# A two-layer RWKV-7 and S5 trunk on one core: the learning rate and the gated unit keep the tanh of their sigmoids, and the half and the offset go into constants and weights

## The chip, the core and the metric

The kernel runs on one core of a Trainium2 chip. A core has a matrix engine (TensorE; PE in the profile, its weight loads PEld), a vector engine (VectorE, DVE), an activation engine (ScalarE, ACT), a general engine (GpSimd, POOL) and a queue that here issues nearly all of the DMAs (SyncE, SP). Each engine runs its own instructions in order and waits on semaphores for the others. The metric is the device time of one execution in microseconds (us), less being better.

## The reference

The input is one sequence of 1024 frames with 1024 features, in float32. Layer 0 mixes over time with RWKV-7, layer 1 with a diagonal complex state-space model and a gated linear unit; each mixer is followed by a squared-ReLU MLP of width 4096, and each of the four sub-layers by a layer norm of sqrt(2)·x + f(x). Cut to what the change touches:

```python
# layer 0, the time mixer
a = jax.nn.sigmoid(a0 + (xa @ a1) @ a2)          # the learning rate
kk = heads(k * k_k)
kk = kk / jnp.maximum(jnp.sqrt(jnp.sum(kk * kk, axis=-1, keepdims=True)), 1e-12)
k = k * (1.0 + (a - 1.0) * k_a)
seq_in = (rh, wh, kh, vh, -kk, kk * ah)
# state = state * w + (state @ a_t) b_t + v k, with a_t = -kk and b_t = kk * a
...
# layer 1, the gated unit
z = y @ w_glu
return z[..., :d] * jax.nn.sigmoid(z[..., d:])
```

## The kernel before

Features lie on the 128 partitions (8 tiles of 128, `KT`), frames on the free axis, in two halves of 512 (`HT`; H is the half). Every large product is made of three float32r products: an operand is split into a high part, a float32r copy that ScalarE makes (`split`, L153), and a low part, the difference, made by VectorE (L154). `mm3` (L201) issues high·high, high·low and low·high. The weights pass through `wload` (L167): a DMA into `wraw`, of which there are two buffers, then the split into `whi` and `wlo`, of which there are three each. The products collect in three PSUM banks (`psd`).

The kernel makes its sigmoids from tanh, as sigmoid(z) = 0.5·tanh(z/2) + 0.5. ScalarE computes the tanh with a scale of 0.5, and a second pass makes the half and the offset.

The time mixer has these steps.

- `rwkv_proj(H)` makes the projections of a half. In it `rates(n)` (L393) makes feature tile n of the decay `sg` and of the learning rate `a`: six small matmuls, then for each of the two a tanh on ScalarE (L404), `half_sigmoid` on ScalarE (L405, its instruction recorded as L349), and a store to DRAM on SP's queue (L406). That is 8 tiles for each half, so 16 times `sg` and 16 times `a`.
- `elem(m)` (L514) makes the operands of the recurrence for m = 0 to 7, a quarter of the frames by half of the features each, in two steps j of 512 columns. It loads k, `sg`, `a` and r from DRAM, normalises `kk`, sums the decay and raises it to E and `cs`. L567 makes 1 + (a - 1)·k_a on ScalarE, as a·k_a + `kam` with `kam` = 1 - k_a from L107; L569 multiplies it with k on GpSimd. L573 writes -kk·E into AR on VectorE, L574 makes kk·a in place of `a` on GpSimd, and L577 and L578 write the two products with `cs` into KB on VectorE, 64 partitions at a time. L579 makes `kf`·r on GpSimd.
- `amat(m)` makes the chunks' matrices from AR and KB, `invert(m)` inverts the triangular ones with many small VectorE products (L652, L654), `chain(m, half)` runs the recurrence, and `gnorm` the norm behind it (GpSimd's L775 among it).

The order comes from a planner: every instruction has a priority, `rank(base)` sets it for a stretch, and a modelled time line puts each engine's instructions in order. The projections of the second half and later the first MLP have lower ranks than the recurrence and fill TensorE between its steps.

In layer 1, `glu(h, ys)` (L1111) runs once for each half, each with 8 output tiles n. It makes the gate's product p2 from the weights `glu[KT + n]`, its tanh (L1116, ScalarE), the half and offset (L1117, one tensor_scalar on GpSimd), then the value's product p1 from the weights `glu[n]`, and multiplies them (L1119) and adds the residual (L1120) on VectorE.

Of the kernel before, what the change touches and what calls it, by code (L numbers as in the profile page):

```python
# [8 lines left out]
F32 = mybir.dt.float32  # L9
F32R = mybir.dt.float32r  # L10
AF = mybir.ActivationFunctionType
ALU = mybir.AluOpType
# [7 lines left out]
KT = 8  # L20
# [49 lines left out]
PV = ["mu0", "mu1", "mu2", "mu3", "mu4", "mu5", "w0", "a0", "k_k", "k_a", "r_k",  # L70
      "g0", "g1", "g2", "g3", "b0", "b1", "b2", "b3", "d", "lb"]


def trunk(ctx, tc, A):
    nc = tc.nc
    V, S, G, PE, SP = nc.vector, nc.scalar, nc.gpsimd, nc.tensor, nc.sync
# [27 lines left out]
    pvh = kp.tile([128, 2, KT], F32, name="pvh")  # L104
    V.tensor_scalar(pvh, pv[:, 6:8], 0.5, None, op0=ALU.mult)
    kam = kp.tile([128, KT], F32, name="kam")
    V.tensor_scalar(kam, pv[:, PV.index("k_a")], -1.0, 1.0, op0=ALU.mult, op1=ALU.add)  # L107

    half = cp.tile([128, 1], F32, name="half")
    V.memset(half, 0.5)  # L110
# [3 lines left out]
    def vec(n, k):  # L114
        i = PV.index(n)
        return pv[:, i, k : k + 1]
# [47 lines left out]

    low = {}

    def wload(src, kt, n, key=None):  # L167

        step = 512 // n
        out = []  # L170
        for k0 in range(0, kt, step):
            kept = low.get((key, k0)) if key else None
            raw = wp.tile([128, step, n], F32, tag="wraw", name="wraw", bufs=2)
            SP.dma_start(raw, src[:, k0 : k0 + step])
            hi = wp.tile([128, step, n], F32R, tag="whi", name="whi")
            lo = wp.tile([128, step, n], F32R, tag="wlo", name="wlo")
            nw[0] += 1
            if kept is not None:
                SP.dma_start(lo.bitcast(F32).rearrange("p k n -> p (k n)"), kept)
                S.copy(hi, raw)  # L180
            else:
                split(raw, hi, lo, G if nw[0] % WLG[0] in WLG[1] and WLG[2] <= nw[0] < WLG[3] else V)
                if key:
                    low[key, k0] = dr.tile([128, 512], F32, name=f"low{len(low)}")
                    SP.dma_start(low[key, k0], lo.bitcast(F32).rearrange("p k n -> p (k n)"))
            out += [(hi[:, k], lo[:, k]) for k in range(step)]
        return out
# [35 lines left out]
    def dense(p, w, xs):  # L223
        n = len(xs)
        for k in range(n):
            mm3(p, w[k][0], w[k][1], xs[k][0], xs[k][1], k == 0, k == n - 1)
# [26 lines left out]
    def rwkv_proj(H):  # L253
# [94 lines left out]
        def half_sigmoid(t):  # L348
            S.activation(t, t, AF.Identity, bias=half, scale=0.5)  # L349
# [43 lines left out]
        def rates(n):  # L393

            if n % 4 == 0:
                w2[0] = wload(A["wa2"][:, n // 4], 4, 128, f"wa2{n}")
            pp = [psd(), psd()]
            for wi, xi in ((0, 0), (0, 1), (1, 0)):
                for j in range(2):
                    js = slice(64 * j, 64 * j + 64)  # L400
                    mmb(pp[j], w2[0][n % 4][wi][js], hx[xi][js], start=wi == 0 and xi == 0, stop=wi == 1)
            for j, out in ((0, "sg"), (1, "a")):
                e = tp.tile([128, HT], F32, tag="ev", name="ev", bufs=EVB)
                S.activation(e, pp[j], AF.Tanh, bias=pvh[:, j, n : n + 1], scale=0.5)  # L404
                half_sigmoid(e)  # L405
                store_out(out, n, e)  # L406

        def gate(n):
# [105 lines left out]
    def elem(m):  # L514
        D = Unit()
        D.m, D.H, D.q, D.t0 = m, m // 4, m % 2, (m // 2) * 256
        D.KB, D.AR, D.o, D.vsa = [], [], {}, {}
        D.bo = kp.tile([128, NC, NP], F32, tag="bo", name="bo", bufs=3)
        D.PL = kp.tile([128, NC, NP], F32, tag="PL", name="PL", bufs=3)
        for j in range(2):  # L520
            n0 = 4 * D.q + 2 * j
            ld = {}
            for nm in ("k", "sg", "a", "r"):
                t = kp.tile([128, 512], F32, tag="ld" + nm, name="ld" + nm, bufs=EB[3] if nm in EB[4] else 1)
                SP.dma_start(t.rearrange("p (i t) -> p i t", i=2),
                             scr[nm][n0 * 128 : n0 * 128 + 256, D.t0 : D.t0 + 256].rearrange("(i p) t -> p i t", p=128))
                ld[nm] = t
            r, k, cs, a = ld["r"], ld["k"], ld["sg"], ld["a"]

            def v3(t):  # L530
                return t.rearrange("p (c l) -> p c l", l=L)

            def per(i):
                return slice(256 * i, 256 * i + 256)

            def ci(t):
                return t[:, :, 2 * j : 2 * j + 2].rearrange("p c i -> p i c")


            sq = kp.tile([128, HT], F32, tag="sq", name="sq", bufs=EB[0])  # L540
            kk = kp.tile([128, HT], F32, tag="kk", name="kk", bufs=EB[1])
            for i in range(2):
                S.mul(kk[:, per(i)], k[:, per(i)], vec("k_k", n0 + i))
            S.activation(sq, kk, AF.Square)
            ps = pa.tile([128, HT], F32, tag="a", name="pss")
            for tt in range(4):
                PE.matmul(ps[:, tt * 2 : tt * 2 + 2], sq[:, tt * 128 : (tt + 1) * 128], hsel, start=True, stop=True)
            rn = kp.tile([128, 8], F32, tag="rn", name="rn", bufs=2)
            V.tensor_scalar(rn, ps[:, 0:8], 1e-24, None, op0=ALU.max)
            G.tensor_tensor(rn, rn, mhalf[:, 0:8], op=ALU.pow)  # L550
            rnb = sq.rearrange("p (t h n) -> p t h n", t=4, h=2)
            S.copy(rnb, rn.rearrange("p (t h) -> p t h", h=2).unsqueeze(3).broadcast_to([128, 4, 2, 64]))
            pn = pa.tile([128, HT], F32, tag="a", name="pn")
            for tt in range(4):
                PE.transpose(pn[:, tt * 128 : (tt + 1) * 128], sq[:, tt * 128 : (tt + 1) * 128], ident)
            V.tensor_mul(kk, kk, pn)

            V.tensor_tensor_scan(cs, cmask.rearrange("p c l -> p (c l)"), cs, 0.0, op0=ALU.mult, op1=ALU.add)
            E = kp.tile([128, 8, L + 1], F32, tag="E", name="E", bufs=EB[5])
            G.memset(E[:, :, 0:1], 1.0)  # L560
            S.activation(E[:, :, 1:], v3(cs), AF.Exp, scale=-DECAY)
            V.tensor_copy(ci(D.PL), E[:, :, L].rearrange("p (i c) -> p i c", i=2))
            S.activation(cs, cs, AF.Exp, scale=DECAY)

            kf = kp.tile([128, HT], F32, tag="kf", name="kf", bufs=EB[2])
            for i in range(2):
                S.activation(kf[:, per(i)], a[:, per(i)], AF.Identity, bias=kam[:, n0 + i : n0 + i + 1],  # L567
                             scale=vec("k_a", n0 + i))
            G.tensor_mul(kf, kf, k)  # L569
            ar = kp.tile([128, 8, 2, L], F32, tag="AR", name="AR", bufs=ARB)  # L570
            kb = kp.tile([128, 8, 2, L], F32, tag="KB", name="KB", bufs=KBB)
            V.tensor_mul(ar[:, :, 1], v3(r), E[:, :, 1:])
            V.scalar_tensor_tensor(ar[:, :, 0], v3(kk), -1.0, E[:, :, 0:L], op0=ALU.mult, op1=ALU.mult)  # L573
            G.tensor_mul(a, kk, a)  # L574
            for h in range(2):
                hs = slice(64 * h, 64 * h + 64)
                V.tensor_mul(kb[hs, :, 1 - h], v3(kf)[hs], v3(cs)[hs])  # L577
                V.tensor_mul(kb[hs, :, h], v3(a)[hs], v3(cs)[hs])  # L578
            G.tensor_mul(kf, kf, r)  # L579
            pb = pa.tile([128, HT], F32, tag="a", name="pb")  # L580
            for c in range(8):
                for h in range(2):
                    hs, bs = slice(64 * h, 64 * h + 64), slice(64 * (1 - h), 64 * (1 - h) + 64)
                    PE.matmul(pb[bs, c : c + 1], kf[hs, c * L : (c + 1) * L], rksel[hs, n0 + c // 4, h : h + 1],
                              start=True, stop=True)
            V.tensor_copy(ci(D.bo), pb[:, 0:8].rearrange("p (i c) -> p i c", i=2))
            D.KB.append(kb)
            D.AR.append(ar)
        return D
# [521 lines left out]
    def glu(h, ys):  # L1111
        for n in range(KT):
            p1, p2 = psd(), psd()
            dense(p2, wload(A["glu"][KT + n], KT, 128), ys)
            s = tp.tile([128, HT], F32, tag="ev", name="sgl", bufs=EVB)
            S.activation(s, p2, AF.Tanh, scale=0.5)  # L1116
            G.tensor_scalar(s, s, 0.5, 0.5, op0=ALU.mult, op1=ALU.add)  # L1117
            dense(p1, wload(A["glu"][n], KT, 128), ys)
            V.tensor_mul(s, s, p1)  # L1119
            V.scalar_tensor_tensor(h[n], h[n], ALPHA, s, op0=ALU.mult, op1=ALU.add)  # L1120


# [478 lines left out]
```

## Time and profile before

| | us |
|---|---|
| median of 3 runs | 2613.07 |
| lowest and highest run | 2607.23, 2613.16 |
| the profiled execution | 2617.01 |
| its span, first to last instruction | 2615.3 |
| mean granted TensorE clock | 0.971 |

In the profile, L12 is line 12 of the kernel. A group of instructions has its engine, its operation and what it writes and reads by the program's names (`ev<-d,pvh`), then how many there were, their busy time and mean duration, and the engine's idle time just before them with what ended it. The chain of waits goes back from the last instruction to what released each step. The granted clock is the share of TensorE's full clock in that stretch. A busy TensorE is not one at its peak, because matmuls overlap each other.

### The profile page before, as it was taken

What the parts mean: (1) busy time and instruction counts of PE and PEld (TensorE: products, weight loads), DVE (VectorE), ACT (ScalarE), POOL (GpSimd) and SP (SyncE); (2) the same over time, 40 slices, a digit from 0 to 9 for tenths busy, and PEclk for the clock granted to TensorE, in tenths of its full rate; (3) what the DMA queues carried; (4) which work ended last, traced back from release to release, by engine and by line L of the source; (5) the groups of instructions that cost most, each with busy time, mean ns of one, the idle gap of its engine ahead of it and who ended that gap; (6) DMA issues with size and microseconds to landing.
All of it is one profiled execution on the core that took longest, in us unless ns stands there. A gap on an engine that the chain in (4) does not pass through costs nothing.

```text
span 2615.3 us, 43837 instructions
## 1 busy us (share of the span) xinstructions
PE 2473.6 (95%) x16624; PEld 2005.4 (77%) x16624; DVE 1813.5 (69%) x3459; ACT 1216.5 (47%) x2171; POOL 443.5 (17%) x372
## 2 busy tenths in 40 slices
PE   7999989999889999999999999999999999999997
PEld 5778767788667888776787888887777888888876
DVE  7366766787986766989886555777587555555576
ACT  7554575654454443345534333433464333433344
POOL 3121432332322001001000000201212111111011
PEclk9998979999989999999999999999999999999998
DMA  4765545554322324445465333253222111111133
GB/s 146 254 219 152 166 162 188 188 190 157 100 74 84 95 85 137 131 129 157 133 227 190 97 97 97 89 190 133 86 88 78 54 47 52 55 51 53 49 96 114
DMA packets 206291, 319.69 MB, mean 122 GB/s; under 512 B 20096, under 2 KB 80640, under 8 KB 206080
## 3 DMA queue, kind: packets, MB, share of 16 engines
q1 hardware_dynamic: 204928, 314.79, 38.2%
q8 instruction: 131, 2.15, 0.3%
q10 hardware_dynamic: 1152, 2.10, 0.2%
q14 instruction: 80, 0.66, 0.1%
HBM read 252.85 MB, written 63.96 MB: 121 GB/s over the span
## 4 chain that ended last, share of the span: by engine, by line
PE 61%; DVE 11%; DMA 3%; issue 2%; ACT 2%; POOL 1%; SPq 0%; ACTq 0%; DVEq 0%; POOLq 0%
PE d L199 46%; PE d L1048 9%; DVE wlo L154 2%; DMA wraw<-in_mw_dram 1%; DVE hA L1011 1%; DMA tt<-tT 1%; PE pA L608 0%; ACT whi L153 0%; PE py L1384 0%; PE pbu L1332 0%; PE pu L1320 0%; PE pk L1281 0%; DVE o L780 0%; DVE sq L891 0%; DVE xh L654 0%
## 5 line engine op out<-in xcount | busy, mean ns | idle before, releaser
L153 ACT CAST whi<-wraw 128x512 fp32r<-128x512 f32 x524 | 324.4, 620 | 680.3 <-PE d L199 465.0
L154 DVE TENSOR_TENSOR wlo<-wraw,whi 128x512 fp32r<-128x512 f32 x524 | 381.3, 728 | 260.2 <-ACT whi L153 255.2
L199 PE MATMUL d<-qbuf,whi 128*128 128x512 f32 (+1 forms) x1344 | 410.3, 389 | 12.8 <-DVE hA L1011 7.8
L199 PE MATMUL d<-oAh,whi 128*128 128x512 f32 (+1 forms) x768 | 308.9, 409 | 16.8 <-ACT ev L429 7.5
L199 PE MATMUL d<-oAh,wlo 128*128 128x512 f32 (+1 forms) x768 | 308.6, 406 | 10.2 <-DVE wlo L154 7.2
L199 PE MATMUL d<-oAl,whi 128*128 128x512 f32 (+1 forms) x768 | 308.0, 404 | 1.4 <-DVE oAl L154 1.4
L199 PEld LDWEIGHTS d<-qbuf,whi 128*128 128x128 f32 x1344 | 245.6, 190 | 67.6 <-DVE hA L1011 11.0
L199 PE MATMUL d<-qbuf,wlo 128*128 128x512 f32 (+1 forms) x672 | 257.2, 385 | 1.3 <-DVE wlo L154 1.1
L199 PE MATMUL d<-oBh,wlo 128*128 128x512 f32 x512 | 203.9, 399 | 3.4 <-DVE wlo L154 3.4
L199 PE MATMUL d<-oBh,whi 128*128 128x512 f32 x512 | 203.1, 397 | 2.4 <-ACT whi L153 2.0
L199 PE MATMUL d<-oBl,whi 128*128 128x512 f32 x512 | 201.4, 393 | 0.0
L199 PEld LDWEIGHTS d<-oAh,whi 128*128 128x128 f32 (+1 forms) x768 | 147.1, 193 | 53.9 <-ACT ev L429 9.7
L199 PEld LDWEIGHTS d<-oAh,wlo 128*128 128x128 f32 (+1 forms) x768 | 146.9, 192 | 46.0 <-DVE wlo L154 10.5
L199 PEld LDWEIGHTS d<-oAl,whi 128*128 128x128 f32 (+1 forms) x768 | 147.4, 193 | 33.3 <-DVE oAl L154 3.0
L199 PE MATMUL d<-qh,wlo 128*128 128x512 f32 x384 | 151.5, 395 | 0.0
L199 PE MATMUL d<-ql,whi 128*128 128x512 f32 x384 | 150.7, 392 | 0.0
L199 PE MATMUL d<-qh,whi 128*128 128x512 f32 x384 | 149.4, 389 | 0.0
L199 PEld LDWEIGHTS d<-qbuf,wlo 128*128 128x128 f32 x672 | 127.2, 190 | 27.9 <-DVE wlo L154 3.2
L1011 DVE TENSOR_TENSOR hB<-hB,d 128x512 f32<-128x512 f32 (+1 forms) x168 | 105.0, 633 | 33.2 <-PE d L199 31.4
L199 PEld LDWEIGHTS d<-oBh,wlo 128*128 128x128 f32 x512 | 96.8, 189 | 27.9 <-DVE wlo L154 4.8
L199 PEld LDWEIGHTS d<-oBh,whi 128*128 128x128 f32 x512 | 97.0, 189 | 24.0 <-ACT whi L153 2.6
L1011 DVE TENSOR_TENSOR hA<-hA,d 128x512 f32<-128x512 f32 x144 | 97.5, 682 | 24.2 <-PE d L199 23.1
(476 smaller groups left out, 5079.2 us busy)
## 6 DMA issues: line engine op xcount, KB each, us to landing
wraw<-in_mw_dram SPq DMA_DIRECT2D x376, 256.0 KB, 2.7
wraw<-in_glu_dram SPq DMA_DIRECT2D x64, 256.0 KB, 2.7
low<-wlo SPq DMA_DIRECT2D x52, 256.0 KB, 2.8
wlo<-low SPq DMA_DIRECT2D x52, 256.0 KB, 3.6
raw<-in_mw_dram SPq DMA_DIRECT2D x48, 256.0 KB, 2.6
wraw<-in_wk_dram SPq DMA_DIRECT2D x32, 256.0 KB, 3.8
wraw<-in_wr_dram SPq DMA_DIRECT2D x32, 256.0 KB, 3.6
wraw<-in_wv_dram SPq DMA_DIRECT2D x32, 256.0 KB, 4.5
```

Source lines behind the costliest of these rows:

```text
L153: S.copy(hi, src)
L154: (e or V).tensor_sub(lo, src, hi.bitcast(F32))
L199: bulk.append((PE.matmul(p, w, x, **kw).ins, x.shape[-1]))
L1011: V.tensor_add(z, z, p)
L1048: PE.matmul(p, w[:, k], x, start=not add and k + j == 0, stop=k == 3 and j == 2, skip_group_check=True)
```

## The change

The learning rate stays tanh: `rates` leaves out `half_sigmoid` for `a`, so what is stored is t = tanh(z/2), with a = 0.5·t + 0.5. In `elem` the factor of the key becomes t·(0.5·k_a) + (1 - 0.5·k_a), from `kam` with another number and a new constant `kah`. The product kk·a becomes (t + 1)·kk in one scalar_tensor_tensor on VectorE, in place of the tensor_mul on GpSimd, and the missing half is a factor in the write of KB, whose tensor_mul becomes a scalar_tensor_tensor.

In the gated unit the tensor_scalar on GpSimd goes. The value's weights are halved in `wload` (a multiplication by 0.5 on ScalarE in place of the copy for the high part, a scalar_tensor_tensor in place of the difference for the low part), and the product becomes (tanh + 1)·p1 in one scalar_tensor_tensor.

```diff
     kam = kp.tile([128, KT], F32, name="kam")
-    V.tensor_scalar(kam, pv[:, PV.index("k_a")], -1.0, 1.0, op0=ALU.mult, op1=ALU.add)
+    V.tensor_scalar(kam, pv[:, PV.index("k_a")], -0.5, 1.0, op0=ALU.mult, op1=ALU.add)
+    kah = kp.tile([128, KT], F32, name="kah")
+    V.tensor_scalar(kah, pv[:, PV.index("k_a")], 0.5, None, op0=ALU.mult)
...
-    def wload(src, kt, n, key=None):
+    def wload(src, kt, n, key=None, halved=False):
...
-            if kept is not None:
+            if halved:
+                S.mul(hi, raw, 0.5)
+                V.scalar_tensor_tensor(lo, raw, 0.5, hi.bitcast(F32), op0=ALU.mult, op1=ALU.subtract)
+            elif kept is not None:
...
                 S.activation(e, pp[j], AF.Tanh, bias=pvh[:, j, n : n + 1], scale=0.5)
-                half_sigmoid(e)
+                if j == 0:
+                    half_sigmoid(e)
                 store_out(out, n, e)
...
                 S.activation(kf[:, per(i)], a[:, per(i)], AF.Identity, bias=kam[:, n0 + i : n0 + i + 1],
-                             scale=vec("k_a", n0 + i))
+                             scale=kah[:, n0 + i : n0 + i + 1])
...
-            G.tensor_mul(a, kk, a)
+            V.scalar_tensor_tensor(a, a, 1.0, kk, op0=ALU.add, op1=ALU.mult)
             for h in range(2):
                 hs = slice(64 * h, 64 * h + 64)
                 V.tensor_mul(kb[hs, :, 1 - h], v3(kf)[hs], v3(cs)[hs])
-                V.tensor_mul(kb[hs, :, h], v3(a)[hs], v3(cs)[hs])
+                V.scalar_tensor_tensor(kb[hs, :, h], v3(a)[hs], 0.5, v3(cs)[hs], op0=ALU.mult, op1=ALU.mult)
...
             S.activation(s, p2, AF.Tanh, scale=0.5)
-            G.tensor_scalar(s, s, 0.5, 0.5, op0=ALU.mult, op1=ALU.add)
-            dense(p1, wload(A["glu"][n], KT, 128), ys)
-            V.tensor_mul(s, s, p1)
+            dense(p1, wload(A["glu"][n], KT, 128, None, True), ys)
+            V.scalar_tensor_tensor(s, s, 1.0, p1, op0=ALU.add, op1=ALU.mult)
             V.scalar_tensor_tensor(h[n], h[n], ALPHA, s, op0=ALU.mult, op1=ALU.add)
```

## The prediction

> **What bounds the kernel now.** I read the page first, then the busy time by stage, then the groups of the lines that the diff touches, then the chain at the places where those lines appear on it.
>
> ```profile
> PE 2473.6 (95%) x16624; PEld 2005.4 (77%) x16624; DVE 1813.5 (69%) x3459; ACT 1216.5 (47%) x2171; POOL 443.5 (17%) x372
> ...
> PE 61%; DVE 11%; DMA 3%; issue 2%; ACT 2%; POOL 1%; SPq 0%; ACTq 0%; DVEq 0%; POOLq 0%
> ```
> ```profile
> 45.00:360.00 315.00, 283.79 (x2275) 229.30 (x2273) 190.77 (x396) 185.70 (x340) 71.58 (x66) 0.92 0.61 196
> 360.00:650.00 290.00, 269.09 (x2784) 223.57 (x2783) 214.24 (x513) 165.54 (x311) 90.75 (x73) 0.94 0.56 179
> 650.00:800.00 150.00, 128.23 (x1160) 102.81 (x1157) 138.10 (x319) 72.14 (x134) 54.25 (x42) 0.90 0.27 83
> 800.00:1660.00 860.00, 840.83 (x5437) 674.97 (x5436) 626.34 (x1182) 372.18 (x658) 51.19 (x40) 1.00 0.42 128
> 1660.00:1810.00 150.00, 145.01 (x1425) 119.23 (x1424) 108.45 (x195) 59.24 (x105) 14.01 (x14) 0.99 0.45 152
> 1810.00:1910.00 100.00, 94.25 (x400) 75.26 (x399) 59.74 (x82) 43.17 (x74) 24.77 (x21) 0.97 0.26 87
> ```
>
> The second fence is the busy time by stage: from:to, length, then busy us and count of PE, PEld, DVE, ACT and POOL, the granted clock, the DMA share and GB/s. TensorE bounds it: 95% busy, 61% of the chain that ended last, against 11% for VectorE, 2% for ScalarE and 1% for GpSimd. The change takes work from ScalarE and GpSimd, so only the places where TensorE waits can pay. In the time mixer, 45 to 800 us, TensorE is idle for 755 - (283.8 + 269.1 + 128.2) = 73.9 us; that is the field. In the last 150 us of it VectorE is busy 138.1 of 150 us (92%) and the granted clock is 0.90: there VectorE is the tight one. In the gated unit (1660 to 1910 us) TensorE is idle for 5.0 + 5.7 us.
>
> **Part 1, the learning rate keeps its tanh.** Of the 32 half-and-offset passes L349 over `ev`, the 16 of the rate `a` go. The first two fences are the view of one line (count, durations as minimum, median and maximum in ns, and who waited); the other two are ScalarE's time line (start, duration).
>
> ```profile
> L404 ACT ACTIVATE ev<-d,pvh x32: 667/680/709, 51.6 to 357.6; 128x512 f32<-128x512 f32 x32
> ```
> ```profile
> L349 ACT ACTIVATE ev<-ev,half x32: 704/718/747, 53.7 to 358.8; 128x512 f32<-128x512 f32 x32
> ...
> who waited for it (us, times):
>   PEld d L199: 0.4, 1
>   PEld pX L721: 0.2, 1
>   PEld pR L716: 0.2, 1
> ```
> ```profile
> 54.87 0.72 ACT L349 ACTIVATE ev<-ev,half 128x512 f32<-128x512 f32 x1
> ...
> 57.13 0.58 ACT L429 COPY ev<-d 128x512 f32<-128x512 f32 x1
> ```
> ```profile
> 336.39 0.71 ACT L349 ACTIVATE ev<-ev,half 128x512 f32<-128x512 f32 x1
> 337.00 0.62 ACT L544 ACTIVATE sq<-kk 128x512 f32<-128x512 f32 x1
> 337.52 0.39 ACT L712 COPY vsa<-st 64x256 f32<-64x256 f32 x1
> ```
>
> 16 x 0.718 = 11.5 us of ScalarE go, all between 50 and 360 us, where it is busy 59% of the time (185.7 of 315). TensorE waited directly for an L349 for only 0.8 us (0.4 + 0.2 + 0.2): PSUM is freed by the tanh L404, which stays. What else can be won is queueing: a pass that stands before a copy that someone needs. The time line shows two such: at 54.9 ahead of L429, which frees a PSUM bank, and at 336.4, where L349 is followed 0.61 us later by the next instruction, and behind both waits L712, which starts a step of the recurrence. I count these two places at 0.6 us each beside the direct waits, and a half of the direct ones as the rate's: -0.4 - 1.2 = **-1.6 us**, from bounds of 0 and -11.5. The store of `a` on SP's queue hangs on L404 now, up to 0.72 us earlier; the queue's order need not change. The added constant `kah` is one more instruction like `kam`, which cost 0.16 us, ahead of the first useful work:
>
> ```profile
> 3.05 0.16 DVE L107 TENSOR_SCALAR kam<-pv 128x8 f32<-128x8 f32 x1
> ```
> ```profile
> 5.07 0.62 ACT L153 CAST oS<-xs 128x512 fp32r<-128x512 f32 x1 [3.00 <-DMA xs<-in_xT_dram]
> ```
>
> ScalarE is waiting for the input until 5.07 us then, so it is hidden; uncovered it would cost 0.16 us.
>
> **Part 2, the product with `kk` goes from GpSimd to VectorE.** First the groups by line (count, busy us, mean ns, idle us before and its releasers), then one undisturbed line, then VectorE's and GpSimd's time lines at two of the sixteen places.
>
> ```profile
> L573 DVE SCALAR_TENSOR_TENSOR AR<-kk,E 128x512 f32<-128x512 f32 x16 | 19.3, 1205 | 0.3
> L574 POOL TENSOR_TENSOR lda<-kk,lda 128x512 f32<-128x512 f32 x16 | 25.4, 1589 | 50.3 <-DVE kk L556 42.2 <-ACT ev L404 6.1 <-DVE x L652 2.0
> L578 DVE TENSOR_TENSOR KB<-lda,ldsg 64x512 f32<-64x512 f32 x32 | 24.4, 763 | 4.7 <-POOL lda L574 4.1 <-DMA gt<-s_g 0.5
> ```
> ```profile
> L1120 DVE SCALAR_TENSOR_TENSOR hA<-hA,sgl x8: 677/686/687, 1676.1 to 1800.9; 128x512 f32<-128x512 f32 x8
> ```
> ```profile
> 761.80 1.29 POOL L574 TENSOR_TENSOR lda<-kk,lda 128x512 f32<-128x512 f32 x1 [6.77 <-DVE kk L556]
> ```
> ```profile
> 761.83 1.80 DVE L573 SCALAR_TENSOR_TENSOR AR<-kk,E 128x512 f32<-128x512 f32 x1
> ```
> ```profile
> 527.10 0.75 DVE L573 SCALAR_TENSOR_TENSOR AR<-kk,E 128x512 f32<-128x512 f32 x1
> 527.26 1.73 POOL L574 TENSOR_TENSOR lda<-kk,lda 128x512 f32<-128x512 f32 x1
> ...
> 529.02 1.39 DVE L578 TENSOR_TENSOR KB<-lda,ldsg 64x512 f32<-64x512 f32 x2 [1.17 <-POOL lda L574]
> ```
>
> An undisturbed scalar_tensor_tensor of 128x512 takes 0.686 us (L1120), so VectorE gets 16 x 0.686 = +11.0 us. But L573 and L574 are both released by the end of `kk`, and the rows show them in each other's way: at 761.8 GpSimd was first and L573 took 1.80 us, ending 0.54 after L574; at 527.1 VectorE was first and L574 took 1.73 instead of 1.29. L573's mean of 1.205 is 0.519 above the undisturbed price, 16 x 0.519 = 8.3 us, and L578 idled 4.1 us for L574. So VectorE's queue changes by between 11.0 - 8.3 - 4.1 = -1.4 (all of the relief comes) and +11.0 us (none). [...]
>
> The two ScalarE passes L567 ahead and the writes of KB (a tensor_tensor turned into a scalar_tensor_tensor) keep their prices. The new product waits in VectorE's queue for what L573 has waited for already, `kk`; of `a` it needs that L567 has read it. What stands behind it are the writes of KB, which need it, and the little products of the inverse (L652 and L654). On the chain of waits (start, us) two of the 16 places count:
>
> ```profile
> 527.30 1.70 POOL lda L574
> ```
> ```profile
> 761.91 1.72 DVE AR L573
> ```
>
> At 527 the product would end at 527.10 + 0.6 + 0.69 = 528.4, not 529.0: -0.6. At 761.9 a blocked 1.72 becomes 0.6 + 0.69, issue to issue, -0.4. Where L573 was not blocked the product is added; with the 11% of the chain that VectorE carries, on half of the relief, 11.0 - 12.4 / 2 = 4.8 us, that is +0.5. Together **-0.5 us**, from -14.4 (each of 16 units shorter by 1.589 - 0.686 = 0.90) to +11.0.
>
> **Part 3, the gated unit.** 16 tensor_scalars on GpSimd go; 32 casts of weights become multiplications, 32 differences become scalar_tensor_tensors. The fences: the view of L1117, of a ScalarE multiplication by a number, the groups of the casts and differences, and a piece of the chain.
>
> ```profile
> L1117 POOL TENSOR_SCALAR sgl<-sgl x16: 618/627/1058, 1664.9 to 1895.5; 128x512 f32<-128x512 f32 x16
> ...
> who waited for it (us, times):
> busy tenths in 40 slices 0000000000000000000000000000000000000000
> ```
> ```profile
> L1249 ACT ACTIVATE b<-bb x1: 627/627/627, 1123.5 to 1123.5; 128x512 f32<-128x512 f32 x1
> ```
> ```profile
> L153 ACT CAST whi<-wraw 128x512 fp32r<-128x512 f32 x524 | 324.4, 620 | 680.3 <-PE d L199 465.0 <-DMA wraw<-in_mw_dram 97.4 <-PE d L1048 23.0
> L154 DVE TENSOR_TENSOR wlo<-wraw,whi 128x512 fp32r<-128x512 f32 x524 | 381.3, 728 | 260.2 <-ACT whi L153 255.2 <-PE d L199 3.0
> ```
> ```profile
> 1822.95 1.09 DVE sq L892
> ```
>
> Nobody waited for L1117: the product that needs it comes after another eight k-steps of TensorE. The removal pays only by clearing VectorE's way, at 1816 and 1823 us, where the chain runs over VectorE and such a pass held it 0.4 us each (the 1.09 of L892 against 0.68): -0.8. A multiplication by a number takes 0.627 (L1249, written as plain f32; none writing f32r is in the trace) against 0.620: +0.2 for 32; at worst the 0.718 of a pass with a bias, +3.1. The difference keeps its price (0.686 against 0.728, both with two SBUF inputs). Sum **-0.6**, from -3 (as much again at the other places) to +3.1.
>
> **Sum.** -1.6 - 0.5 - 0.6 = -2.7 us. The profiled execution took 2617.0 us (span 2615.3), 3.9 above the median 2613.07 of the runs shown, which spread from 2607.2 to 2613.2; it would become 2614.3, and the median 2610.4.
>
> **Rivals.**
> *The GpSimd step was the length of the recurrence* (chance 0.22). The chain elem, matrix, inverse, recurrence is as long as its slowest link; if TensorE's 73.9 idle us hang on it, each of the 16 units gains 0.90, 14.4, and with part 1 16 us: 2597. For it: 4.1 us of waits of L578 and 9.2 of L543 on L574. Against: L574 is on the chain once.
> *VectorE takes its place* (0.20): the slower side. Other GpSimd work moves up into L574's slot (L775 with its 2.89 us, below, runs right behind the L574 of that unit), so L573 stays blocked, and all 16 products lie in the queue of the engine that is 92% busy from 650 to 800 us. Price 11.0 on the path, less 1.6 and 0.6: +8.8, 2622. It decides if L573's mean stays near 1.2 us. [...]
>
> ```profile
> 706.20 2.89 POOL L775 TENSOR_TENSOR vt<-vsa,bo 64x512 f32<-64x512 f32 x2
> ```
>
> *The multiplied casts are dearer than casts* (0.04): +3.1 in place of +0.2, 2613.
>
> **Chances.** The forecast has 0.54. A measurement of this kernel tells about 0.3% (8 us) from no change. The first rival gives faster, the second slower, and the planner's new order may carry the forecast over either edge: faster 0.26, same 0.53, slower 0.21. The range takes in both rivals' centres, 2597 to 2622, and leaves out their outer halves, 0.2.
>
> **What would show it.** Right: L573 near 0.7 us, the new product near 0.7 to 0.9, no wait of KB for GpSimd, GpSimd's busy time lower by 25 + 12 us, ScalarE's by 11, TensorE's idle time from 45 to 800 us within some us of 73.9. Wrong: L573 still near 1.2 (second rival), idle time of TensorE down by over 8 us (first), casts at 0.72 us (third), or a granted clock from 45 to 800 us that differs from 0.92, 0.94 and 0.90, which I hold fixed.

## The result and the profile after

| | before | after |
|---|---|---|
| median, us (14 runs each, side by side) | 2613.11 | 2605.15 |
| lowest and highest run, us | 2603.31, 2622.60 | 2597.55, 2612.68 |
| ratio after / before, 95% interval | | 0.9969 [0.9956, 0.9983] |
| the profiled execution, us | 2617.01 | 2612.68 |
| its mean granted clock | 0.971 | 0.967 |

The change is worth -0.31%, 8.0 us, with an interval from 0.17 to 0.44%. That is 5 us below the forecast of 2610.4. By the mark that the prediction set for what can be told from no change, about 0.3% or 8 us, it lies at the edge between "the same" and "faster". The medians in this document are of all runs, and the ratios leave out three slow ones: 3422.14 us (before, in group e below), 10255.29 (f1) and 3978.37 (g3).

The profiled execution of the changed kernel is the longest of its 14 runs, and that of before lies 4 us above its median, so the two pages are 4.3 us apart and not 8.

First the page of the changed kernel: its span, the busy time of each engine, and the chain that ended last.

```profile
span 2610.9 us, 43753 instructions
...
PE 2475.1 (95%) x16624; PEld 2008.2 (77%) x16624; DVE 1814.7 (70%) x3476; ACT 1205.8 (46%) x2155; POOL 411.9 (16%) x340
...
PE 70%; DVE 13%; DMA 8%; ACT 4%; issue 3%; POOL 1%; SPq 1%; ACTq 0%; DVEq 0%; POOLq 0%
```

The span of a TensorE-bound kernel splits into TensorE's busy and idle time. Before, it was 2615.3 = 2473.6 + 141.7; after, it is 2610.9 = 2475.1 + 135.8. GpSimd lost 31.6 us of busy time (443.5 to 411.9) and ScalarE 10.7 (1216.5 to 1205.8), and TensorE's idle time fell by 5.9. The chains can't be compared by their shares: those of before add up to 80%, those of after to 100%, so the chain of before seems to have been followed back over part of the span only.

Next, the changed kernel's busy time by stage, with the columns of the same view in the prediction.

```profile
45.00:360.00 315.00, 288.75 (x2378) 233.82 (x2378) 205.45 (x426) 183.03 (x339) 67.50 (x62) 0.92 0.62 201
360.00:650.00 290.00, 265.12 (x2649) 220.30 (x2645) 206.62 (x514) 158.14 (x297) 79.00 (x64) 0.92 0.56 175
650.00:800.00 150.00, 128.31 (x1185) 102.87 (x1184) 131.19 (x289) 71.39 (x134) 47.65 (x38) 0.87 0.26 79
800.00:1660.00 860.00, 845.03 (x5448) 679.41 (x5447) 628.73 (x1198) 373.05 (x659) 53.40 (x41) 0.99 0.41 128
1660.00:1810.00 150.00, 146.15 (x1430) 119.83 (x1429) 108.77 (x198) 61.09 (x108) 8.42 (x6) 0.99 0.45 153
1810.00:1910.00 100.00, 95.74 (x420) 77.26 (x419) 64.45 (x89) 46.38 (x80) 21.77 (x15) 1.00 0.27 87
```

In the time mixer (45 to 800 us), where the prediction looked for the gain, TensorE's idle time is 755 - (288.75 + 265.12 + 128.31) = 72.8 us, against 73.9: nothing moved there. It fell from 19.2 to 15.0 us between 800 and 1660, where the source differs in nothing, and from 10.7 to 8.1 in the gated unit. The three clocks of the mixer are 0.92, 0.92 and 0.87, against 0.92, 0.94 and 0.90.

Last, the groups of the changed lines. The numbers have moved: the write of AR is L579, the new product L580, the half's write of KB L584, the half-and-offset pass L354, the halved weights L181 and L182.

```profile
L579 DVE SCALAR_TENSOR_TENSOR AR<-kk,E 128x512 f32<-128x512 f32 x16 | 12.3, 766 | 0.1
L580 DVE SCALAR_TENSOR_TENSOR lda<-lda,kk 128x512 f32<-128x512 f32 x16 | 13.8, 866 | 0.0
...
L584 DVE SCALAR_TENSOR_TENSOR KB<-lda,ldsg 64x512 f32<-64x512 f32 x32 | 21.9, 683 | 0.2
...
L354 ACT ACTIVATE ev<-ev,half 128x512 f32<-128x512 f32 x16 | 11.5, 721 | 0.0
...
L181 ACT ACTIVATE whi<-wraw 128x512 fp32r<-128x512 f32 x32 | 20.2, 630 | 46.0 <-PE d L204 34.5 <-DMA wraw<-in_glu_dram 9.4 <-DVE sb L884 2.1
...
L182 DVE SCALAR_TENSOR_TENSOR wlo<-wraw,whi 128x512 fp32r<-128x512 f32 x32 | 23.1, 722 | 8.5 <-ACT whi L181 8.5
```

Locally the change does what was foretold. AR's write is nearly free of GpSimd (1205 to 766 ns). The half's write of KB no longer waits for it (4.7 us of waits to 0.2) and is faster itself (763 to 683 ns). Together with the new product's 13.8 us, VectorE's queue changes by 12.3 - 19.3 + 13.8 + 21.9 - 24.4 + 0.2 - 4.7 = -0.2 us: the exchange is even. At two of the sixteen places, though, what the prediction's second rival told of happens: `gnorm`'s product on GpSimd (L781, before the change L775; at the first of them also L897 behind it, from 710.81 us) runs beside the two instructions and both take longer. AR's write has a median of 688 ns and took 1531 ns and 1.11 us at these places; the new product has a median of 685 ns and took 2744 at the first of them, 1527 at the second.

```profile
L580 DVE SCALAR_TENSOR_TENSOR lda<-lda,kk x16: 678/685/2744, 108.3 to 795.8; 128x512 f32<-128x512 f32 x16
```

The question is where 8 us come from then.

### The profile page after: what moved, and what is told of

The parts are those of the page before. It is cut to its first block, busy times and chain, and to the rows that moved or that the text cites. A ratio compares the mean times of both kernels' runs of the same rounds, so it can differ in the third digit from the quotient of the medians.

```text
span 2610.9 us, 43753 instructions
## 1 busy us (share of the span) xinstructions
PE 2475.1 (95%) x16624; PEld 2008.2 (77%) x16624; DVE 1814.7 (70%) x3476; ACT 1205.8 (46%) x2155; POOL 411.9 (16%) x340
## 4 chain that ended last, share of the span: by engine, by line
PE 70%; DVE 13%; DMA 8%; ACT 4%; issue 3%; POOL 1%; SPq 1%; ACTq 0%; DVEq 0%; POOLq 0%
PE d L204 52%; PE d L1054 9%; DVE wlo L156 2%; DMA wraw<-in_mw_dram 2%; PE pA L614 1%; DMA ldsg<-s_sg 1%; ACT whi L155 1%; PE pU L732 1%; PE pR L722 1%; DVE oAl L156 1%; PE pO L743 1%; PE pO L741 1%; DVE KB L584 1%; PE pX L727 0%; DMA s_y<-yg 0%
## 5 line engine op out<-in xcount | busy, mean ns | idle before, releaser
L155 ACT CAST whi<-wraw 128x512 fp32r<-128x512 f32 x492 | 304.6, 620 | 634.6 <-PE d L204 438.6
L156 DVE TENSOR_TENSOR wlo<-wraw,whi 128x512 fp32r<-128x512 f32 x492 | 356.3, 724 | 242.3 <-ACT whi L155 236.7
```

The source lines that it names most:

```text
L155: S.copy(hi, src)
L156: (e or V).tensor_sub(lo, src, hi.bitcast(F32))
```

## The experiments

Eight theories were set against each other; their letters stand in the expectations.

- **A**: small local terms as in the prediction, a few us in all. **B**: the product on GpSimd was the length of the recurrence. **C**: the ScalarE passes of the rate cost by queueing.
- **D**: the planner's order counts, not the work: any edit gives another order of the whole program, and the time goes with that.
- **E**: the gain is in the gated unit. **F**: it takes parts 1 and 2 together. **G**: it is the gated unit's GpSimd pass, which holds VectorE. **H**: the gated unit's gain comes from its new order.

The runs fall into three groups, e, f and g, each on another chip. Each group has 12 runs of each of its kernels and 35 of the kernel before, whose medians were 2612.03 (e), 2613.98 (f) and 2611.67 (g). A ratio is to the runs of before in the same group. It lies nearer to the quotient of the means than to that of the medians, which can be apart where runs scatter.

### Each part alone

e1, the learning rate alone, with the product left on GpSimd. It leaves out the + 1 of the product, and its constants are the change's:

```diff
-                half_sigmoid(e)
+                if j == 0:
+                    half_sigmoid(e)
...
-                             scale=vec("k_a", n0 + i))
+                             scale=kah[:, n0 + i : n0 + i + 1])
...
             G.tensor_mul(a, kk, a)
...
-                V.tensor_mul(kb[hs, :, h], v3(a)[hs], v3(cs)[hs])
+                V.scalar_tensor_tensor(kb[hs, :, h], v3(a)[hs], 0.5, v3(cs)[hs], op0=ALU.mult, op1=ALU.mult)
```

> Part 1 alone: the rate is stored as tanh, the constants are halved, the product with kk stays a tensor_mul on GpSimd (so the + 1 of the product is left out and b is 0.5 kk tanh), the gated unit is as before. Theory A (the prediction's terms, each small): 1.6 us faster than before, no difference that can be measured. Theory B (the GpSimd product was the length of the recurrence): no difference either, since it stays. Theory C (16 ScalarE passes of 0.72 us stood ahead of things that TensorE waits for): 6 to 11 us faster. Theory D (what counts is the new order that the planner makes, not the work): anything within 6 us either way, and the parts do not add up to the whole's 8 us.

e2, the product alone, on VectorE, with the sigmoid kept:

```diff
-            G.tensor_mul(a, kk, a)
+            V.tensor_mul(a, kk, a)
```

> Part 2 alone: the sigmoid stays, the product of kk and a is a tensor_mul on VectorE instead of GpSimd; everything else as before. Theory A: 0.5 us faster, not to be measured; the group of AR<-kk,E falls from 1205 ns to about 770. Theory B: 6 to 14 us faster, most of the whole's gain. Theory C: within 2 us of before. Theory D: within 6 us either way.

e3, the gated unit alone, with `wload` as in the change:

```diff
-            G.tensor_scalar(s, s, 0.5, 0.5, op0=ALU.mult, op1=ALU.add)
-            dense(p1, wload(A["glu"][n], KT, 128), ys)
-            V.tensor_mul(s, s, p1)
+            dense(p1, wload(A["glu"][n], KT, 128, None, True), ys)
+            V.scalar_tensor_tensor(s, s, 1.0, p1, op0=ALU.add, op1=ALU.mult)
```

> Part 3 alone: the gated unit with halved weights and tanh + 1, the time mixer as before. Theory A: 0.6 us faster. Theories B and C: within 1 us of before. A fourth reading of the profile, E: the last output of the gated unit came 6.9 us earlier and the time mixer's last step 1.3 us later in the changed kernel's profile, so the gain lies behind 1050 us; by it this kernel is 4 to 8 us faster alone. Theory D: within 6 us either way.

e4, both parts of the mixer as in the change, without the gated unit (two of its places are shown):

```diff
-                half_sigmoid(e)
+                if j == 0:
+                    half_sigmoid(e)
...
-            G.tensor_mul(a, kk, a)
+            V.scalar_tensor_tensor(a, a, 1.0, kk, op0=ALU.add, op1=ALU.mult)
```

> Parts 1 and 2 together, the changed kernel with the gated unit of before. Theory A: 2.1 us faster than before. Theories B and C: the whole 8 us. Theory E: within 2 us of before. Theory D: not the sum of the runs with part 1 and part 2 alone, by 4 us or more.

| | median, us | ratio to before, 95% interval |
|---|---|---|
| e1 rate alone | 2613.63 | 1.0007 [0.9995, 1.0020] |
| e2 product alone | 2612.85 | 1.0011 [0.9998, 1.0024] |
| e3 gated unit alone | 2610.14 | 0.9996 [0.9984, 1.0008] |
| e4 rate and product | 2609.86 | 0.9985 [0.9962, 1.0008] |

None can be told from no change. B asked for 6 to 14 us of e2, and 1.0011 bears no gain over 0.02%. Yet e2 has all of the local relief, as its groups show (here the write of AR is L573, the product L574, KB's write from `lda` L578):

```profile
L578 DVE TENSOR_TENSOR KB<-lda,ldsg 64x512 f32<-64x512 f32 x32 | 21.9, 683 | 0.2
...
L574 DVE TENSOR_TENSOR lda<-kk,lda 128x512 f32<-128x512 f32 x16 | 13.7, 859 | 0.0
L573 DVE SCALAR_TENSOR_TENSOR AR<-kk,E 128x512 f32<-128x512 f32 x16 | 11.1, 695 | 0.2
```

The 8.2 us that AR's write won (19.3 to 11.1), and the 4.5 us of waits of KB, are paid back by the product's 13.7, and neither side reaches TensorE's path by more than the interval can hide. C asked for 6 to 11 us of e1, which takes away 11.5 us of ScalarE: its interval ends at a gain of 1.3. E asked for 4 to 8 us of e3, whose interval ends at 4.2.

These verdicts hold the order of the instructions at nothing, and the runs below show that it isn't: orders of the same work lie up to 0.5%, some 13 us, apart. A new order in e1 or e2 can hide a gain of some us. B's full 14 us would need a dearer order than any seen here; the lower ends of B and C are made unlikely by these runs, but not excluded by them alone.

### Two parts at a time, the change again, and an order alone

f1 is e1's and e3's edits together (again without the + 1), f2 is e2's and e3's; f5 is the changed kernel once more, beside them. f3 is the kernel before with the two rates of a feature tile made in the other order; no work goes or comes:

```diff
-            for j, out in ((0, "sg"), (1, "a")):
+            for j, out in ((1, "a"), (0, "sg")):
```

> Parts 1 and 3: the changed kernel with the product of kk left to GpSimd (a tensor_mul; the + 1 of the product is left out). The order of the time mixer is that of the run with part 1 alone, so the difference to that run is part 3's. Theory A: 2.2 us faster than before if the clock is granted alike; since the run with part 1 alone had 0.9665 of the clock against 0.9689, about 1 us faster is measured. Theory E (the gated unit alone brings it): 4 to 8 us faster than the run with part 1 alone. Theory F (parts 1 and 2 are worth something only together, because the ScalarE time that part 1 frees is used only when the GpSimd product goes too): no faster than before by more than 2 us.

> Parts 2 and 3: the sigmoid of the rate stays on ScalarE, the product of kk is a tensor_mul on VectorE, the gated unit is the changed one. The order of the time mixer is that of the run with part 2 alone. Theory A: 1.1 us faster than before. Theory E: 4 to 8 us faster than the run with part 2 alone. Theory F: within 2 us of before.

> The kernel before with one loop turned round: the tanh of the rate is issued ahead of that of the decay. No work is added or removed, but the planner puts all engines in another order from the first recurrence on. Theory D (the order counts, not the work): off from before by 3 us or more in either direction, with another granted clock. Theories A, B and E: within 2 us of before.

> The changed kernel once more, beside the others of this call. Theory A (terms of 1.6, 0.5 and 0.6 us): 2 to 5 us faster than before, a little slower than its first measurement, which would have been on the lucky side of its interval. Theories B to F: the 8 us again. It also gives part 3 as the difference to the run with parts 1 and 2, whose time mixer has the same order.

| | median, us | ratio to before, 95% interval |
|---|---|---|
| f1 rate and gated unit | 2611.03 | 0.9990 [0.9975, 1.0005] |
| f2 product and gated unit | 2611.23 | 0.9988 [0.9973, 1.0002] |
| f3 before, rates turned | 2615.38 | 1.0000 [0.9982, 1.0018] |
| f5 the change again | 2605.91 | 0.9972 [0.9954, 0.9990] |

The change's gain is there again (0.9972), and every pair has less of it. Each part with and without the gated unit gives four pairs with the same order of the mixer on TensorE: e3 against before, f1 against e1, f2 against e2, f5 against e4. By the ratios they differ by -0.04, -0.17, -0.23 and -0.13%, in the mean -0.14%, some 4 us. If the printed intervals are taken as independent, the mean's own is about ±0.11 (an estimate), so 1 to 6 us. So a part of the gain, perhaps half, seems to lie in the gated unit, though no pair by itself is told from nothing, and three of the four compare runs of different groups. F asked for no gain over 2 us in f1 and f2; they have 2.6 and 3.1, with intervals that hold 0, and so leave it open. f3 moved nothing, which spoke against D, as one new order out of many can.

That the orders are as said can be read from the traces, by the place of each matmul in TensorE's list, by operation and tiles. All the kernels have the same 16624 matmuls. Within the four pairs the lists differ at 48 to 52 places, of which 2 to 6 are ahead of 1640 us; two executions of the changed kernel differ at 8. f3's list differs from that of before at 6671 places.

The page of f5's profiled execution:

```profile
span 2603.0 us, 43753 instructions
...
PE 2469.5 (95%) x16624; PEld 2006.2 (77%) x16624; DVE 1817.3 (70%) x3476; ACT 1206.3 (46%) x2155; POOL 411.4 (16%) x340
```

This is the same program as in the first section, 7.9 us shorter: 5.6 less of busy TensorE and 2.3 less idle. What separates two profiles of different kernels by less than that says nothing.

### Orders turned, and the GpSimd pass put back

g1 is f3's turn of the rates, in the changed kernel. g2 is the changed kernel with the two writes of KB turned, g3 the kernel before with the same turn:

```diff
-                V.tensor_mul(kb[hs, :, 1 - h], v3(kf)[hs], v3(cs)[hs])
                 V.tensor_mul(kb[hs, :, h], v3(a)[hs], v3(cs)[hs])
+                V.tensor_mul(kb[hs, :, 1 - h], v3(kf)[hs], v3(cs)[hs])
```

g4 is the changed kernel with a pass on GpSimd between the gate's tanh and the value's product, where the one of before stood. It multiplies by one, so it costs the time and keeps the values:

```diff
+            G.tensor_scalar(s, s, 1.0, 0.0, op0=ALU.mult, op1=ALU.add)
             dense(p1, wload(A["glu"][n], KT, 128, None, True), ys)
```

> The changed kernel with the loop over decay and rate turned round, as in the run of the kernel before with that loop turned: the same work, another order on every engine from the first recurrence on. Theory F (the work taken from ScalarE and GpSimd together is what gains): 6 to 9 us faster than before, like the changed kernel. Theory D (its gain above part 3's 3.6 us is one lucky order): back at 2 to 5 us faster than before, or off by 3 us or more to either side of the changed kernel.

> The changed kernel with the two writes of KB in the other order (the product with a ahead of the product with the key's factor): the same work, another order from 368 VectorE instructions on. Theory F: 6 to 9 us faster than before. Theory D: 2 to 5 us faster, or off from the changed kernel by 3 us or more.

> The kernel before with the two writes of KB in the other order: the product with a, which waits for GpSimd, now stands ahead. Theory F: within 2 us of before, or slower, since VectorE then waits for GpSimd before it can do the other write. Theory D: off from before by 3 us or more to either side.

> The changed kernel with a GpSimd pass over the gate's tanh put back, times 1 plus 0, in the place where the half and the offset were made; the weights stay halved. TensorE and ScalarE have exactly the changed kernel's order. Theory G (the GpSimd pass holds VectorE up, and its going is part 3's 3.6 us): 3 to 4 us slower than the changed kernel, so 4 to 5 us faster than before. Theory H (part 3's gain comes from the new order of the layer norms and weights): as fast as the changed kernel within 1.5 us.

| | median, us | ratio to before, 95% interval |
|---|---|---|
| g1 changed, rates turned | 2617.29 | 1.0019 [1.0008, 1.0031] |
| g2 changed, keys turned | 2619.26 | 1.0024 [1.0013, 1.0036] |
| g3 before, keys turned | 2606.87 | 0.9965 [0.9952, 0.9978] |
| g4 changed, pass put back | 2604.64 | 0.9973 [0.9956, 0.9989] |

**The order counts, as D says.** g3 takes no work away and gains as much as the change: two lines of the kernel before, turned. Its ratio says -0.35%; by the medians it is 4.8 us, by the means 7.8. g1 and g2 have all of the change's savings and are slower than the kernel before, which A has no room for, and for which F foretold a gain of 6 to 9 us. Their lists of matmuls differ from those of the kernels that they were made from at 4245 (g3), 7587 (g1) and 4381 places (g2). D gave a size and no direction: which order would win, nothing here foretold. The page and the write of AR in g3:

```profile
span 2599.1 us, 43831 instructions
...
PE 2468.6 (95%) x16624; PEld 2000.5 (77%) x16624; DVE 1816.0 (70%) x3459; ACT 1217.2 (47%) x2171; POOL 447.5 (17%) x372
```
```profile
L573 DVE SCALAR_TENSOR_TENSOR AR<-kk,E 128x512 f32<-128x512 f32 x16 | 20.1, 1254 | 0.3
```

GpSimd still has its 447.5 us and AR's write still takes its 1254 ns, against 695 in e2, and the kernel is fast all the same: in this order, those costs lie beside the path. TensorE is idle for 2599.1 - 2468.6 = 130.5 us here, against 141.7 before. In g2 it is idle for 2617.1 - 2471.6 = 145.5:

```profile
span 2617.1 us, 43749 instructions
...
PE 2471.6 (94%) x16624; PEld 2004.3 (77%) x16624; DVE 1822.8 (70%) x3476; ACT 1206.7 (46%) x2155; POOL 413.2 (16%) x340
```

A piece of that can be named. The view of TensorE's waits (who waited, for what: us in all, times, longest) has at its head in g2, and further down in the changed kernel, the matmuls that make the chunks' matrices (L614), waiting for their PSUM bank to be emptied into AT:

```profile
PE pA L614 <- DVE AT L618: 18.8, 9, 4.5
```
```profile
PE pA L614 <- DVE AT L618: 3.4, 2, 1.8
```

They are 15.4 us apart in single executions, in a line that the change doesn't touch and with the same instructions in both. It is the order's and not the execution's: in f5 and g4, which have the changed kernel's order, the same line has 4.5 and 2.5 us. Part of it came back elsewhere: by the busy time from 45 to 800 us, first of g2, then of g1, TensorE idles for 83.4 us in g2 and for 67.8 in g1, against 72.8 in the changed kernel.

```profile
45.00:800.00 755.00, 671.58 (x6143) 548.22 (x6143) 543.79 (x1217) 412.13 (x766) 189.33 (x160) 0.92 0.52 166
```
```profile
45.00:800.00 755.00, 687.24 (x6226) 561.68 (x6225) 542.57 (x1206) 416.96 (x773) 199.41 (x164) 0.91 0.53 167
```

So g1's loss is not in the mixer's waits, as far as this execution shows: it is the shortest of g1's 12 (2613.33, median 2617.29), and from 800 to 1660 us TensorE idles in it for 22.0 us, against 15.0 in the changed kernel. g1's mean granted clock over its runs is 0.9667, against 0.9697 of before in that group. At the 1.3 us for each thousandth that the last section gives, that would be some 4 of the 5.6 us by which its median is longer; it is an estimate and no cause shown. For the changed kernel it is another thing: f5's mean clock is 0.9689 and that of before 0.9690, so f5's gain of 8 us is not the clock's.

g4 was to decide between G and H. Its order on TensorE and ScalarE is that of the changed kernel, instruction by instruction, and on VectorE a few instructions near 1845 us stand otherwise, so little but the pass differs:

```profile
L1123 POOL TENSOR_SCALAR sgl<-sgl 128x512 f32<-128x512 f32 x16 | 11.8, 735 | 143.6 <-ACT sgl L1122 143.6
```

With its 11.8 us back on GpSimd the kernel has a ratio of 0.9973, against 0.9969 and 0.9972 without. The intervals of some 4 us to either side can't exclude the 3 to 4 us that G asked for. The traces tell a little more. In g4 the unit runs from the start of its first tanh, 1656.3, to the end of its last residual, 1891.4 + 0.7:

```profile
L1122 ACT ACTIVATE sgl<-d x16: 575/591/600, 1656.3 to 1884.8; 128x512 f32<-128x512 f32 x16
```
```profile
L1126 DVE SCALAR_TENSOR_TENSOR hB<-hB,sgl x8: 679/685/1800, 1809.9 to 1891.4; 128x512 f32<-128x512 f32 x8
```

That is 235.7 us. Measured alike, it took 233.5 to 237.8 us, in the mean 234.9, in the six executions with the unit of before (before, e1, e2, e4, f3, g3), and 232.6 to 234.6, in the mean 233.2, in the seven with the changed one (after, e3, f1, f2, f5, g1, g2). So the unit itself is some 1.7 us shorter, at the lower end of what the pairs gave, and with the pass back g4's single execution has the length of before. G, at that smaller size, isn't out, and H, the unit's new order, isn't shown.

Does the work count at all? Three orders of each kernel have been measured. The changed work gives -0.28, +0.19 and +0.24%, in the mean +0.05. The work of before gives 0, 0.00 and -0.35%, in the mean -0.12. Three orders are few, but they give no sign that what was taken away is worth anything that can be measured, while the orders of one and the same work lie up to 0.5% apart.

**What stays open.** Why one order is better than another is shown only in pieces (L614's wait in g2, and an estimate of the clock's part in g1); TensorE's idle time alone doesn't give the ranking, as f1's execution had 131.7 us of it at a ratio of 0.9990, with a busy time of 2478.2. And the change's 8 us are not split between the mixer (e4, 0.9985, an interval that holds 1) and the gated unit, nor the gated unit's part between the pass on GpSimd and the new order.

## Why the prediction was right or wrong

The time fell into the range, 5 us below the forecast, and the likeliest case, little or nothing, is what the parts gave one by one. The reasoning held in its local steps; the sum lacked its largest term. That the time came out below that of before, as forecast, was in large part luck: the same work in the orders of g1 and g2 took 0.19 and 0.24% longer than before, which the range would have held as well.

- **What bounds the kernel.** Right: TensorE is 95% busy before and after, and taking 10.7 us from ScalarE and 31.6 from GpSimd (25 + 12 were foretold) shows no gain by itself.
- **Part 1, -1.6 us.** e1 gives 1.0007 [0.9995, 1.0020], that is between -1.3 and +5.2 us, which just leaves out -1.6; but e1 has an order of its own, which can hide more than that, so the term is neither shown nor refuted. The two queueing places were read out of one execution's time line, and a new order puts other instructions there. That the passes were hidden is right.
- **Part 2, -0.5 us.** The local terms are right: AR's write fell from 1205 to 766 ns, KB's wait for GpSimd went, and VectorE's queue came out even (-0.2 us, inside the -1.4 to +11.0 given for it). e2 gives 1.0011 [0.9998, 1.0024], -0.5 to +6.3 us, in which -0.5 just lies; a term of this size is below what an order moves.
- **Part 3, -0.6 us.** The casts are right: 630 ns foretold as 627, the differences 722 against 728. The reason given for a gain was the GpSimd pass clearing VectorE's way at 1816 and 1823 us; g4 puts a pass back and shows no longer time, but its gated unit took 235.7 us, against 232.6 to 234.6 without the pass. A gain of this kind, -0.8 or somewhat more, is neither shown nor excluded.
- **First rival, the GpSimd step as the length of the recurrence.** 14.4 us were asked for, and e2's interval ends at a gain of 0.5; g1 and g2 have the step gone as well and are slower than before.
- **Second rival, VectorE takes its place.** It was to decide by L573's mean staying near 1.2 us; it fell to 766, and e2 and e4 show no 11 us. What it told of is there at two of the sixteen places, where AR's write and the new product run beside L781 and take 1531 and 2744 ns at the worse one, against medians of 688 and 685. That the work on GpSimd holds VectorE up is borne out by the rows (1205 ns in the mean for AR's write with L574 on GpSimd, 695 in e2 without it); by what mechanism, they don't show. It didn't set the time, though: g3 has it in full (1254 ns) and is faster than before.
- **The step that failed.** The sum treated the program as fixed but for the edited lines. "The planner's new order may carry the forecast over either edge" stood among the chances and had no term: it was held at nothing, and the granted clock was held at 0.92, 0.94 and 0.90. The runs put that term at -0.35 to +0.24% around the kernel before, -9 to +6 us, two to three times the sum of -2.7. The signs for "right" were met (idle time of the mixer 72.8 against 73.9), and so was one for "wrong", the clock of the mixer, with 0.92, 0.92 and 0.87. The 8 us that came weren't in the terms of the sum.

## What to carry to other kernels

Where a planner lays out the instructions anew at every edit and one engine is 95% busy, test a small edit beside edits that change only the order: here two turned lines gave all of the change's gain, and the change with the same two lines turned lost it. Put a term of both signs for the new order into a forecast, as large as such controls are apart. Here one of two other orders of the kernel before gained as much as taking work off two engines that aren't the bound.

## What the runs showed of the hardware

**The clock was withheld in whole steps of 3.41 us, also where TensorE had been busy for a third of the step before.** Here are five neighbouring stretches of the kernel before and two later ones, each one step long, in the view of busy time by stretch (columns as above).

```profile
1842.47:1845.89 3.42, 3.42 (x17) 2.76 (x15) 2.20 (x3) 3.42 (x6) 2.83 (x2) 1.00 0.22 77
1845.89:1849.30 3.41, 1.08 (x4) 0.30 (x2) 1.58 (x1) 3.41 (x8) 3.41 (x4) 1.00 0.00 0
1849.30:1852.71 3.41, 1.51 (x4) 1.24 (x5) 3.41 (x3) 1.47 (x3) 3.41 (x3) 0.51 0.13 38
1852.71:1856.13 3.42, 3.42 (x10) 2.68 (x9) 3.42 (x5) 1.20 (x2) 2.29 (x2) 0.50 0.33 115
1856.13:1859.54 3.41, 3.41 (x16) 2.81 (x15) 2.00 (x5) 0.66 (x2) 0.00 (x0) 0.99 0.34 95
1941.49:1944.90 3.41, 1.14 (x6) 0.64 (x5) 3.41 (x5) 3.41 (x8) 1.62 (x2) 1.00 0.00 0
1944.90:1948.31 3.41, 3.41 (x10) 2.63 (x9) 3.41 (x5) 3.33 (x7) 1.64 (x1) 0.50 0.29 77
```

A stretch with TensorE busy for 1.08 of 3.41 us is followed by one at a clock of 0.51; that one has 1.51 of 3.41 busy and is followed by one at 0.50; this second one is full (3.42), and behind it the clock is back at 0.99. At 1941 a stretch with 1.14 us busy is followed by one at 0.50, 95.60 us or 28 steps of 3.414 us after the one at 1846. All the clock records of this execution's trace but the last are whole multiples of 3.413 us long, those at half the clock one to five steps (3.41 to 17.07 us). The full stretches above have 10 matmuls at 0.50, 16 or 17 at 0.99 and 1.00. In the changed kernel's execution the steps begin at other times: a stretch at 0.50 begins at 1778.62 us, and the first one below 64.86 us or 19 steps later. There a wait of TensorE of 2.20 us, from 1846.01 to 1848.21, is shared by two stretches, and these and the next are at 1.00:

```profile
1843.48:1846.89 3.41, 1.87 (x7) 0.88 (x6) 3.12 (x4) 3.30 (x7) 3.41 (x3) 1.00 0.01 2
1846.89:1850.31 3.42, 2.10 (x9) 1.76 (x10) 3.42 (x3) 0.00 (x0) 3.42 (x3) 1.00 0.23 76
1850.31:1853.72 3.41, 2.42 (x12) 1.66 (x11) 2.45 (x3) 0.63 (x1) 0.70 (x1) 1.00 0.13 40
```

So 2.33 us of idle time inside one stretch (3.41 - 1.08) were followed by two stretches at 0.51 and 0.50, and a wait of 2.20 us that lay in two stretches by none. A stretch at half the clock costs up to 1.7 us (an estimate from the length of 3.41 us and the 0.50). That it goes by where a wait falls on the steps is the author's estimate from these two places. How much of a stretch must be busy was not shown: from 405.51 to 408.92 us of the kernel before TensorE is busy for all of 3.41 us, and the stretch behind is at 0.50. It would be a way in which an order of the same work gets another time; that it makes the differences between the orders here was not shown.

**One kernel's executions differ by more than the change is worth.** The 14 runs of the kernel before span 19.3 us (2603.31 to 2622.60), those of the changed one 15.1. In group g a run of before at a mean clock of 0.975 took 2603.52 us and one at 0.966 took 2621.91, about 2 us for each thousandth of the clock between these two. A straight line through all 35 runs of before in that group gives 1.3.
